# A hybrid decoder layer: one more projection unit in the fourth query blocks, and all gate chunks of a branch ahead of its products

## The chip, the cores and the metric

The kernel runs on one core of a Trainium2 chip. The metric is the device time of one execution in microseconds (us); before the change three runs gave a median of 1011.76 us, from 1009.65 to 1013.55. One more execution was profiled; its own time is given below.

## What is computed

One decoder layer of 512 tokens and width 1024, in float32, with a final RMSNorm. Cut to what matters here:

```
h = rms_norm(x)
fq, fk, fv, f_logit, dq, dk, dv, gate_a, gate_b = split(h @ w_in)
y_a = fox attention (8 heads of 64, causal, bias from the cumulative forget gate)
y_b = differential attention (4 heads: softmax(q1 k1) - lam * softmax(q2 k2), rotary q and k)
merged = sigmoid(gate_a) * (y_a @ w_branch_a) + sigmoid(gate_b) * (y_b @ w_branch_b)
x = x + merged @ w_out
x = x + cross_attention(rms_norm(x), rms_norm(mem))
x = x + mixture of 32 experts, 2 of 8 in one of 4 groups (SwiGLU, 512 wide)
out = rms_norm(x)
```

## The kernel before

The program is written in the order in which every engine carries it out: PE, DVE, ACT, POOL and the DMA queue of SP each take their instructions in the order of the text and wait only for semaphores. TensorE (PE) computes most products in three passes (high times high, high times low, low times high, lines 266 to 268), for which each weight is split in a high part (ACT, line 165) and a low part (POOL, or DVE for a few, line 166).

The first half is the mixer. All that is a projection of h is cut into *units*: one unit is 24 matmuls into one PSUM bank, with 128 columns of a weight chunk and all 512 tokens (`t_unit`, line 298), or 48 smaller ones (`nat_unit`, line 283). A unit returns its evacuation as a function, which is called later. The units stand in one list (lines 856 to 897), in the order: fox values, fox queries and keys of the second group (`fox_unit`), rotary queries and keys of the differential heads (`rope_unit`) with their values between, then for each branch its gate units (`gate_unit`, line 815) and its products (`branch_unit`, line 829: 12 matmuls with the attention's result). Before the change the order in a branch is two gate chunks (four units), four products, two gate chunks, four products; in branch B the memory's key/value units (`kv_unit`) stand ahead of the last four. The units of branch B also finish the merge: their evacuation takes L839 (gate times product) and L846 (sum of the two branches) on DVE, L849 on ACT and L850 on DVE.

The attention runs in 24 blocks (line 907): 16 of fox (four pairs of heads, four query blocks each; block 0 to 15) and 8 differential (two groups, four query blocks each; block 16 to 23). The query block b reads (b+1)*128 keys, so the fourth (b = 3, blocks 3, 7, 11, 15, 19, 23) is the longest. A block goes so (lines 918 to 963): scores on PE; softmax on DVE and ACT; whatever a rope unit left over (`late`: two matmuls with a swap matrix, L639 and L640, and its DVE and ACT steps); a unit; the product of the block before with its values; the combine step on DVE (L582 to L585, for differential L686 to L692), which scales the probabilities; the split of the next weight half (`W.more`); then the transposes of the probabilities on PE (L263) and their copies. In a differential block a second unit stands ahead of the transposes: the evacuation of the first is called there, then its rest, then the unit:

```
        if isinstance(it, Diff):
            ev()
            while late:
                late.pop(0)()
            ev = unit()
            W.more()
        it.trans()
```

PSUM banks come from three tags (line 74): units, rope rests and the transposes of the differential output (L738) share "a" with two banks; scores and transposes share "s" with four; "y" has two. SBUF is handed out in pages of 8 KB a partition, NPG = 18 of them (line 29): inputs, weights and results of the mixer, and later the experts' weights, which are fetched in a ring of 15 pages (`Experts`, line 1242) and two more tiles.

After the attention come the rest of the units (line 977), the output product (`out_unit`, line 999), the cross-attention, the router, and from about 520 us the loop over 16 pairs of experts (line 1553).

Of the kernel before, what the change touches and what calls it, by code (L numbers as in the profile page):

```python
# [21 lines left out]
NT = S // P  # L22
# [3 lines left out]
CAP = 64  # L26
QUAD = 4
NEG = -1.0e30
NPG = 18
NLD = 3  # L30
NPG2 = 4
RING = 15
# [6 lines left out]
def tile_hybrid_block(  # L39
# [7 lines left out]
    cp = ctx.enter_context(tc.tile_pool(name="cp", bufs=1))  # L47
    pgp = ctx.enter_context(tc.tile_pool(name="pgp", bufs=NPG))
    ps = ctx.enter_context(tc.tile_pool(name="ps", bufs=1, space=bass.MemoryType.PSUM))
# [6 lines left out]
    def page(shape, dt, name):  # L56
        return pgp.tile(list(shape), dt, name=name, tag="pg")
# [15 lines left out]
    def bank(name, tag):  # L73
        return ps.tile([P, 512], F32, name=name, tag=tag, bufs={"a": 2, "s": 4, "y": 2}[tag])
# [93 lines left out]
    W = Stream()  # L168

    def wcols(col):  # L170

        return W.add(w_inp[(col - 8 * (col > 1536)) // 256].rearrange("p (k n) -> p k n", k=KD), KD, 256)
# [97 lines left out]
    def gemm(o, nk, lh, ll, rh, rl):  # L270
        for k in range(nk):
            mm3(o, lh(k), ll(k), rh(k), rl(k), k == 0, k == nk - 1)
# [480 lines left out]
    def mem_load():  # L753
        M["x"] = page([P, 2, D], F32, "mt")
        nc.sync.dma_start(M["x"], mem[0].rearrange("(t p) d -> p t d", p=P))
        M["g"] = gvec(g_mem, "gb_mem")

    def mem_stat():
        ss = tiny([P, 2], "nm_ss")
        for t in range(2):  # L760
            junk = work([P, D], BF, f"nm{t}_j")
            A.activation(junk, M["x"][:, t], AF.Square, accum_out=ss[:, t:t + 1])
        M["r"] = rsqrt(ss, 2, 1.0 / D, 1e-6, "nm")

    def mem_norm(t):
        M["xn", t] = xn = big(f"nm{t}_n")
        V.scalar_tensor_tensor(xn, M["x"][:, t], M["r"][:, t:t + 1], M["g"], op0=OP.mult, op1=OP.mult)

    def mem_trans(t):
        if t == 0:  # L770
            M["h"] = page([P, KD, MEM], F32R, "mth")
            M["l"] = page([P, KD, MEM], F32R, "mtl")
        sl = slice(t * P, (t + 1) * P)
        for q in range(2):
            pt = bank(f"tm{t}{q}", "s")
            t4(pt, M["xn", t][:, q * 512:(q + 1) * 512])
            split(M["h"][:, 4 * q:4 * q + 4, sl], M["l"][:, 4 * q:4 * q + 4, sl],
                  pt.rearrange("p (a b) -> p a b", b=P))
        return None
# [3 lines left out]
    def kv_unit(i, j):  # L783
        if "k" not in M:
            M["k"] = page([P, 4, MEM], F32R, "kch")
            M["v"] = c2.tile([P, 2, MEM], F32, name="cv")
        wh, wl = W.use(c_kv[i], j)
        o = bank(f"kv{i}{j}", "a")[:, 0:256]
        sl = slice(j * P, (j + 1) * P)
        if i == 0:  # L790
            gemm(o, KD, lambda k: wh[:, k, sl], lambda k: wl[:, k, sl], lambda k: M["h"][:, k, :],
                 lambda k: M["l"][:, k, :])
        else:
            gemm(o, KD, lambda k: M["h"][:, k, sl], lambda k: M["l"][:, k, sl], lambda k: wh[:, k, :],
                 lambda k: wl[:, k, :])
        if i == 0:
            return lambda: split(M["k"][:, j], M["k"][:, 2 + j], o)
        return lambda: A.activation(M["v"][:, j], o, AF.Copy)

    wbr = [w[0].rearrange("(k p) n -> p k n", p=P) for w in (w_branch_a, w_branch_b)]  # L800
    c_ga, c_wa, c_gb, c_wb = [], [], [], []
    for c in range(4):
        c_ga.append(wcols(3080 + 256 * c))
        if c % 2 == 1:
            c_wa.append(W.add(wbr[0][:, :, 256 * (c - 1):256 * (c + 1)], 4, 512))
    for c in range(4):
        c_gb.append(wcols(4104 + 256 * c))
        if c == 3:
            for i in range(2):
                c_kv[i] = W.add(ckv[:, :, 256 * i:256 * i + 256], KD, 256)  # L810
        if c % 2 == 1:
            c_wb.append(W.add(wbr[1][:, :, 256 * (c - 1):256 * (c + 1)], 4, 512))
    GT = {}

    def gate_unit(br_, c, j):
        key = (br_, c // 2)
        if key not in GT:
            GT[key] = page([P, 4, S], F32, f"g{br_}{c // 2}")
        d = GT[key][:, 2 * (c % 2) + j]

        def evac(j, o):
            V.tensor_tensor(d, o, RT, op=OP.mult)
            A.activation(d, d, AF.Tanh, scale=0.5)

        return t_unit((c_ga, c_gb)[br_][c], j, evac, f"w{br_}{c}")
# [3 lines left out]
    def branch_unit(br_, c, j):  # L829

        wh, wl = W.use((c_wa, c_wb)[br_][c], j // 2)
        YH, YL = (YAH, YAL) if br_ == 0 else (YB["h"], YB["l"])
        o = bank(f"br{br_}{c}{j}", "a")
        sl = slice(j * P, (j + 1) * P)
        gemm(o, 4, lambda k: wh[:, k, sl], lambda k: wl[:, k, sl], lambda k: YH[:, k, :], lambda k: YL[:, k, :])

        def evac():
            ga = GT[br_, c][:, j]
            V.scalar_tensor_tensor(ga, ga, 1.0, o, op0=OP.add, op1=OP.mult)  # L839
            if br_ == 0:  # L840
                return
            if not MH:
                for i in range(2):
                    MH[i] = page([P, KD, S // 2], F32R, f"mh{i}")
                    ML[i] = page([P, KD, S // 2], F32R, f"ml{i}")
            V.tensor_tensor(ga, ga, GT[0, c][:, j], op=OP.add)  # L846
            for i in range(2):
                sl = slice(i * S // 2, (i + 1) * S // 2)
                A.activation(MH[i][:, 4 * c + j], ga[:, sl], AF.Copy, scale=0.5)  # L849
                V.scalar_tensor_tensor(ML[i][:, 4 * c + j], ga[:, sl], 0.5, MH[i][:, 4 * c + j].bitcast(F32),  # L850
                                       op0=OP.mult, op1=OP.subtract)

        return evac


    units = []
# [22 lines left out]
    for br_ in range(2):  # L879
        for c in range(4):  # L880
            for j in range(2):
                if (br_, c) == (1, 3):
                    units.append(lambda j=j: mem_trans(j))
                units.append(lambda br_=br_, c=c, j=j: gate_unit(br_, c, j))
            if (br_, c) == (0, 3):
                units.append(lambda: mem_load())
            if (br_, c) == (1, 0):
                units.append(lambda: mem_stat())
            if (br_, c) in ((1, 1), (1, 2)):
                units.append(lambda c=c: mem_norm(c - 1))  # L890
            if (br_, c) == (1, 3):
                for i in range(2):
                    for j in range(2):
                        units.append(lambda i=i, j=j: kv_unit(i, j))
            if c % 2 == 1:
                for j in range(4):
                    units.append(lambda br_=br_, c=c, j=j: branch_unit(br_, c // 2, j))
    wov = w_out[0].rearrange("(k p) n -> p k n", p=P)
    c_wo = [W.add(wov[:, :, 256 * c:256 * c + 256], KD, 256) for c in range(4)]
    c_cq = W.add(w_cq[0].rearrange("(k p) n -> p k n", p=P), KD, 256)  # L900
# [17 lines left out]
    for n, it in enumerate(its):  # L918
        it.scores()
        it.soft()  # L920
        while late:
            late.pop(0)()
        fe = rows() if rows is not None else None
        ev = unit()
        if fe is not None:
            fe()
        fin2 = prev.av() if prev is not None else None
        if n == 1:
            swap_matrix()
        if n == 2:  # L930
            rotary_angles()
        if n == 3:
            rotary_tables()
        if n == 4:
            lam_calc()
        if n == 5:
            rotary_spread()
        if n == 7:
            dv = page([P, NT, 512], F32, "dv")
        it.combine()  # L940
        if fin is not None and isinstance(done, Diff):
            done.scale()
        W.more()
        if isinstance(it, Diff):
            ev()
            while late:
                late.pop(0)()
# [4 lines that stand above are left out]
            it.copy()  # L952
            ev()
        else:
            ev()
            it.copy()
        rows = fin
        if isinstance(it, Fox) and it.b == NT - 1 and it.pr < 3:
            Fox(it.pr + 1, 0).prep()
        if n == 15:  # L960
            YB["h"] = page([P, 4, S], F32R, "ybh")
            YB["l"] = page([P, 4, S], F32R, "ybl")
        done, prev, fin = prev, it, fin2
# [807 lines left out]
```

## Time and profile before

| | us |
|---|---|
| median of three runs | 1011.76 |
| lowest, highest | 1009.65, 1013.55 |
| the profiled execution | 1016.84 |
| its span (first to last instruction) | 1015.1 |

In the profile PE is TensorE's matmuls, PEld its weight loads, DVE is VectorE, ACT ScalarE, POOL GpSimd and SP the engine whose queue issues the DMAs. "L692" is line 692 of the kernel. An idle mark at the end of a row, such as `[1.01 <-DVE T L692]`, tells how long the engine stood idle ahead of this instruction and what ended that. PEclk is the granted share of TensorE's full clock of 2.4 GHz.

### The profile page before, as it was taken

The page shows a single profiled execution, that of the slowest core. Times are in us where ns is not written, and L with a number is a line of the kernel's source. Part 1 is how long each engine was busy: PE and PEld are TensorE (multiplying, and loading weights), DVE is VectorE, ACT ScalarE, POOL GpSimd, SP SyncE. Part 2 cuts the span into 40 slices and gives each one's busy share as a digit, 9 for nine tenths or more (in the row PEclk, how much of TensorE's full clock was granted, in tenths as well). Part 3 has the DMA queues.
Part 4 walks back from the last instruction along what each step waited for, and adds up shares of the span by engine and source line. Part 5 has one row for each costly group of instructions (what it writes and reads, how often), then busy time and mean ns, then how long its engine had stood idle before and what let it go on. Part 6 is the DMA issues. An engine that isn't in the chain of part 4 may idle for free. (4 is left out here: it accounts for less than half of the span.)

```text
span 1015.1 us, 13870 instructions
## 1 busy us (share of the span) xinstructions
PE 968.5 (95%) x5494; PEld 643.9 (63%) x5495; DVE 453.9 (45%) x966; ACT 307.7 (30%) x670; POOL 195.9 (19%) x244
## 2 busy tenths in 40 slices
PE   7999899999999999999899999999999999999985
PEld 6687677787877888898656536354363635436332
DVE  5455685846563535445632333322333332233334
ACT  5334344434352344345421202121021212112104
POOL 3840222233343455610100000000000000000003
PEclk9999999999899999999999999999999999999998
DMA  8121121112132228336479899999999999999902
GB/s 305 63 84 63 42 62 64 63 63 81 45 115 86 90 85 270 122 126 274 183 279 419 314 423 421 421 421 418 421 422 421 422 420 421 420 421 420 409 18 83
DMA packets 47575, 246.19 MB, mean 243 GB/s; under 512 B 4625, under 2 KB 12049, under 8 KB 23441
## 3 DMA queue, kind: packets, MB, share of 16 engines
q1 hardware_dynamic: 47360, 245.03, 61.0%
q8 instruction: 45, 0.74, 0.3%
q14 instruction: 26, 0.20, 0.1%
q10 hardware_dynamic: 144, 0.21, 0.1%
HBM read 243.13 MB, written 2.10 MB: 242 GB/s over the span
## 5 line engine op out<-in xcount | busy, mean ns | idle before, releaser
L1403 PE MATMUL gu<-gu,xg 128*64 128x512 f32 x960 | 210.5, 593 | 1.7 <-PEq L1472 1.6
L166 POOL TENSOR_TENSOR wl<-wr,wh 128x1024 fp32r<-128x1024 f32 x50 | 120.4, 2414 | 194.2 <-ACT wh L165 187.0
L1403 PEld LDWEIGHTS gu<-gu,xg 128*64 128x64 f32 x960 | 72.8, 137 | 133.3 <-issue 118.6
L1425 PE MATMUL yd<-dn,A 128*64 128x512 f32 x472 | 110.4, 596 | 0.0
L1447 DVE TENSOR_TENSOR xr<-cb,xr 128x512 f32<-128x512 f32 x120 | 75.7, 685 | 50.7 <-PE cb L1443 50.5
L1408 DVE SCALAR_TENSOR_TENSOR A<-A,gu 128x256 f32<-128x256 f32 x32 | 13.5, 421 | 176.1 <-ACT A L1407 176.1
L1543 POOL MEMSET A<- 128x128 f32 x1 | 0.2, 205 | 438.2 <-PE pth L263 438.2
L1425 PEld LDWEIGHTS yd<-dn,A 128*64 128x64 f32 x472 | 34.9, 137 | 64.4 <-issue 63.4
L1407 ACT ACTIVATE A<-gu 128x256 f32<-128x256 f32 x32 | 12.3, 383 | 200.7 <-PE gu L1403 200.7
L165 ACT ACTIVATE wh<-wr 128x1024 fp32r<-128x1024 f32 x64 | 66.8, 1050 | 7.7 <-POOL wr L135 6.8
L1443 PE MATMUL cb<-Y,ohT 128*128 128x512 f32 x240 | 66.7, 408 | 0.9
L1433 DVE SCALAR_TENSOR_TENSOR Y<-yd,ws,Y 128x512 fp32r<-128x512 f32 x32 | 23.9, 751 | 91.8 <-ACT Y L1432 89.9
L1231 PE MATMUL ga<-G,hnh 128*128 128x256 f32 x256 | 64.6, 290 | 0.2 <-DVE ge L1351 0.2
L1231 PE MATMUL ga<-G,hnl 128*128 128x256 f32 x256 | 62.8, 283 | 0.0
L1432 ACT ACTIVATE Y<-yd,ws 128x512 fp32r<-128x512 f32 x32 | 21.9, 687 | 126.9 <-PE yd L1425 126.9
L1231 PEld LDWEIGHTS ga<-G,hnh 128*128 128x128 f32 x256 | 48.6, 190 | 3.1 <-issue 2.4
L1443 PEld LDWEIGHTS cb<-Y,ohT 128*128 128x128 f32 x240 | 42.1, 189 | 12.3 <-DVE xr L1447 3.4
L1231 PEld LDWEIGHTS ga<-G,hnl 128*128 128x128 f32 x256 | 48.6, 190 | 0.6
L1377 ACT ACTIVATE xg<-ga,smc 128x256 f32<-128x256 f32 x64 | 29.8, 474 | 52.3 <-PE ga L1231 52.3
L266 PE MATMUL wop<-wh,mh 128*128 128x256 f32 x128 | 36.9, 288 | 3.0 <-DVE xr L1011 1.8
L267 PE MATMUL wop<-wl,mh 128*128 128x256 f32 x128 | 36.4, 284 | 0.5 <-POOL wl L166 0.5
L268 PE MATMUL wop<-wh,ml 128*128 128x256 f32 x128 | 36.4, 284 | 0.0
(611 smaller groups left out, 1958.8 us busy)
## 6 DMA issues: line engine op xcount, KB each, us to landing
gu<-in_w_gu_dram SPq DMA_DIRECT2D x120, 1024.0 KB, 12.1
dn<-in_w_dn_dram SPq DMA_DIRECT2D x55, 1024.0 KB, 17.2
wr<-in_w_inp_dram SPq DMA_DIRECT2D x40, 512.0 KB, 3.7
Z<-in_w_gu_dram SPq DMA_DIRECT2D x8, 1024.0 KB, 14.6
wr<-in_w_out_dram SPq DMA_DIRECT2D x8, 512.0 KB, 5.6
Z<-in_w_dn_dram SPq DMA_DIRECT2D x4, 1024.0 KB, 19.8
dn<-in_w_dn_dram SPq DMA_DIRECT2D x6, 512.0 KB, 13.9
xT<-in_x_t_dram SPq DMA_DIRECT2D x4, 512.0 KB, 6.8
```

What stands on the lines that cost most here:

```text
L165: A.activation(hi, src, AF.Copy)
L166: E.tensor_tensor(lo, src, hi.bitcast(F32), op=OP.subtract)
L266: PE.matmul(o, lh, rh, start=first, stop=False)
L267: PE.matmul(o, lh, rl, start=False, stop=False)
L268: PE.matmul(o, ll, rh, start=False, stop=last)
L1231: PE.matmul(o, CX[u, t // 2][:, t % 2, kb * P:(kb + 1) * P], GQ[q][:, t].rearrange("p e s -> p (e s)"), start=(first and u == "h"), stop=( ...
L1377: A.activation(XG[q][:, kb], o, AF.Copy, scale=gfc[:, kb:kb + 1])
L1403: PE.matmul(gu[64 * f:64 * f + 64, :], xg(2 * i + j), w[:, :, j, 256 * f:256 * f + 256], start=(i + j == 0), stop=(i + j == 4))
L1425: PE.matmul(y[j][64 * a:64 * a + 64, :], hT[a][:, f % 2, f // 2], w(a, f)[:, j, f % 2], start=(f == 0), stop=(f == 3))
L1433: V.scalar_tensor_tensor(yl[rows, j], y[j][rows], ws, yh[rows, j].bitcast(F32), op0=OP.mult, op1=OP.subtract)
L1443: PE.matmul(banks[j], oh[:, t * P:(t + 1) * P], y[u][:, j], start=(u == 0), stop=(u == 1))
L1447: V.tensor_tensor(xs, banks[j], xs, op=OP.add)
```

## The change

Three things. A fourth query block of either kind goes once more through the step that stood in differential blocks alone: evacuation, rest, unit, split. So fourth fox blocks have two units between scores and transposes and fourth differential blocks three. The list of units (and of weight chunks, which must agree) has all four gate chunks of a branch ahead of its eight products. And there is one page more, since more gate results are alive at once.

```diff
-NPG = 18
+NPG = 19
...
     for c in range(4):
         c_ga.append(wcols(3080 + 256 * c))
-        if c % 2 == 1:
-            c_wa.append(W.add(wbr[0][:, :, 256 * (c - 1):256 * (c + 1)], 4, 512))
+    for c in range(2):
+        c_wa.append(W.add(wbr[0][:, :, 512 * c:512 * c + 512], 4, 512))
     for c in range(4):
         c_gb.append(wcols(4104 + 256 * c))
         if c == 3:
             for i in range(2):
                 c_kv[i] = W.add(ckv[:, :, 256 * i:256 * i + 256], KD, 256)
-        if c % 2 == 1:
-            c_wb.append(W.add(wbr[1][:, :, 256 * (c - 1):256 * (c + 1)], 4, 512))
+    for c in range(2):
+        c_wb.append(W.add(wbr[1][:, :, 512 * c:512 * c + 512], 4, 512))
...
-            if c % 2 == 1:
+            for c2_ in ((), (0, 1))[c == 3]:
                 for j in range(4):
-                    units.append(lambda br_=br_, c=c, j=j: branch_unit(br_, c // 2, j))
+                    units.append(lambda br_=br_, c=c2_, j=j: branch_unit(br_, c, j))
...
-        if isinstance(it, Diff):
+
+        for _ in range(isinstance(it, Diff) + (it.b == NT - 1)):
             ev()
             while late:
                 late.pop(0)()
```

## Rows read from the trace of the kernel before

**Rows 1.** The page: busy us, share of span, instructions; PE's slices in tenths.
```profile
PE 968.5 (95%) x5494; PEld 643.9 (63%) x5495; DVE 453.9 (45%) x966; ACT 307.7 (30%) x670; POOL 195.9 (19%) x244
...
PE   7999899999999999999899999999999999999985
```
**Rows 2.** Stretches: us, busy of PE PEld DVE ACT POOL, clock, DMA share, GB/s.
```profile
600.00:650.00 50.00, 50.00 (x269) 24.20 (x266) 13.00 (x25) 8.64 (x18) 0.00 (x0) 1.00 1.01 421
```
**Rows 3.** Order of time, PE, block 19: start us, us, engine, line, op, [idle before].
```profile
243.26 0.40 PE L666 MATMUL sd<-maskb,identb 128*128 128x128 bf16 x4
...
247.72 0.47 PE L266 MATMUL br<-yah,wh 128*128 128x512 f32 x1
...
250.34 0.39 PE L268 MATMUL br<-yah,wl 128*128 128x512 f32 x1
251.74 0.63 PE L263 MATMUL td<-identf,T 128*128 128x128 f32 x4 [1.01 <-DVE T L692]
252.93 0.63 PE L263 MATMUL td<-identf,T 128*128 128x128 f32 x4 [0.56 <-DVE T L692]
```
**Rows 4.** Order of time, PE, end of block 23 and behind it.
```profile
304.20 0.63 PE L263 MATMUL td<-identf,T 128*128 128x128 f32 x4 [1.04 <-DVE T L692]
...
306.48 0.66 PE L738 MATMUL tz<-identf,zn 128*128 128x128 f32 x4 [0.48 <-DVE g L839]
307.68 0.50 PE L266 MATMUL br<-yah,wh 128*128 128x512 f32 x1 [0.54 <-DVE g L839]
```
**Rows 5.** Order of time, PE: block 7 (three rows), blocks 11 and 15.
```profile
118.87 0.39 PE L266 MATMUL dq0p<-hh,wh 128*128 128x512 f32 x1
...
124.40 0.88 PE L607 MATMUL yo<-pf,fv 128*64 128x128 f32 x12
...
126.23 0.66 PE L263 MATMUL tf<-identf,S 128*128 128x128 f32 x4 [0.36 <-DVE S L585]
...
161.17 1.09 PE L263 MATMUL tf<-identf,S 128*128 128x128 f32 x8
...
196.74 0.66 PE L263 MATMUL tf<-identf,S 128*128 128x128 f32 x4 [0.31 <-DVE S L585]
```
**Rows 6.** Stretches behind blocks 15, 19 and 23; the clock is third from the end.
```profile
199.10:202.50 3.40, 3.40 (x17) 3.21 (x18) 2.79 (x10) 1.77 (x9) 0.00 (x0) 0.50 0.05 18
...
253.70:260.50 6.80, 6.80 (x29) 5.60 (x28) 4.83 (x17) 2.67 (x10) 0.00 (x0) 0.50 0.05 18
...
308.30:311.70 3.40, 3.40 (x10) 2.63 (x9) 0.65 (x1) 0.00 (x0) 1.74 (x1) 0.50 0.11 19
```
**Rows 7.** Order of time, DVE, combine of block 19 and the next evacuation.
```profile
248.67 2.92 DVE L692 SCALAR_TENSOR_TENSOR T<-T,dr,T 128x512 f32<-128x512 f32 x1
...
252.03 0.75 DVE L692 SCALAR_TENSOR_TENSOR T<-T,dr,T 128x512 f32<-128x512 f32 x1
...
253.30 0.68 DVE L839 SCALAR_TENSOR_TENSOR g<-g,br 128x512 f32<-128x512 f32 x1
```
**Rows 8.** Order of time, POOL, block 19.
```profile
248.67 2.38 POOL L166 TENSOR_TENSOR wl<-wr,wh 128x1024 fp32r<-128x1024 f32 x1 [3.28 <-DVE T L691]
```
**Rows 9.** Order of time, DVE, evacuation of block 7's rope unit.
```profile
126.09 0.68 DVE L166 TENSOR_TENSOR dqk0l<-dq0p,dqk0h 128x512 fp32r<-128x512 f32 x1
126.69 0.68 DVE L635 TENSOR_TENSOR r001a<-dq0p,rot 128x512 f32<-128x512 f32 x1
```
**Rows 10.** Order of time, PE, transposes of the third blocks 6 and 14.
```profile
116.85 0.55 PE L263 MATMUL tf<-identf,S 128*128 128x128 f32 x3 [1.13 <-DVE S L585]
...
187.43 0.55 PE L263 MATMUL tf<-identf,S 128*128 128x128 f32 x3 [0.79 <-DVE S L585]
```
**Rows 11.** Branch B's evacuation: a group (busy us, mean ns, idle), an instruction in time.
```profile
L846 DVE TENSOR_TENSOR g<-g,g 128x512 f32<-128x512 f32 x8 | 13.9, 1732 | 0.3
...
398.46 0.76 DVE L850 SCALAR_TENSOR_TENSOR ml<-g,mh 128x256 fp32r<-128x256 f32 x2 [0.48 <-ACT mh L849]
```
**Rows 12.** Order of time, PE, the output product behind branch B.
```profile
399.87 0.39 PE L266 MATMUL wop<-wh,mh 128*128 128x256 f32 x1 [0.55 <-DVE g L839]
```

## The prediction

> **What bounds the kernel now.** I read the page first. TensorE (PE) is busy 95% of the span, and its row of slices is at nine tenths nearly everywhere [rows 1]. So a change pays only where it takes away PE idle time or slow PE clock. Then I looked at the second half by stretches: in 600 to 650 us, which stands for all of 525 to 950, PE is busy 50.00 of 50 us while the DMA engines are also full (1.01, 421 GB/s) [rows 2]. There the weights stream just fast enough, and PE never stops. The change touches nothing that PE does there, so whatever the attention part wins or loses moves the end by the same amount.
>
> Then I went through PE's own order of time in the attention part (58 to 316 us) and wrote down each idle mark and what ended it. Blocks are numbered 0 to 23 in the order of the loop; 3, 7, 11 and 15 are the fourth query blocks of fox, 19 and 23 those of the differential heads. In block 19 the scores end at 243.66, two branch products of 3.0 us each run (247.72 to 250.73 is the second), and then PE waits 1.01 us for the first transposes and 0.56 us for the second [rows 3]. Both waits end with DVE at L692. Block 23 repeats this (1.04, and again 0.56), and loses 0.48 and 0.54 us more just behind it, waiting for L839 on DVE [rows 4]. In fox, block 7 waits 0.36 and block 15 0.31 us, block 11 nothing [rows 5]. The stretches give the other loss: after blocks 15, 19 and 23 the granted clock is 0.5, which is 1.2 instead of 2.4 GHz, for 3.4, 6.8 and 3.4 us, with PE busy all the time [rows 6]. Half of that is lost: 1.7 + 3.4 + 1.7 = 6.8 us. So what the change aims at is 1.6 + 2.6 + 0.7 us of waiting and up to 6.8 us of slow clock, 11.7 us, of which it has to pay its own costs.
>
> **Why DVE is late there.** The combine step's L692 took 2.92 us in block 19; the same instruction on the other half took 0.75 [rows 7]. Next to it POOL ran the weight split of the next unit, from 248.67 to 251.05 [rows 8]. The long one ended half a microsecond behind the split's end. The Trainium skill, SBUF — State Buffer, "Who interferes with whom", has a rule for this: DVE's second port is GpSimd's, it is an exclusive lock, and the loser stands until the other's instruction is over. The trace agrees (2.92 against 0.75 us). By that rule the extra unit speaks against itself in part, because each new weight half brings another such split.
>
> **The change part by part.**
>
> *Block 23 and what is behind it.* Now three units stand between scores and transposes, and by the new order they are three gate units; a unit of 24 matmuls takes 5.5 us (118.87 to 124.40) [rows 5]. The last combine ends 9.1 us behind the scores (243.66 to 252.78 in block 19 [rows 3, 7]), and the first two gate units alone take 11. So all four waits go, 1.04 + 0.56 + 0.48 + 0.54 = 2.62 us. I leave 0.2 for the wait of the next unit on the third one's evacuation: **-2.4**.
>
> *Block 19.* Here the three units are products of branch A, 3.0 us each, and the third is not free to start. Projections share two PSUM banks (tag "a"), so the third needs the bank of the first. The first is emptied by L839, and DVE works in order: in the code that step stands behind combine. In the trace it ran from 253.30 to 253.98, behind L692 and the scaling [rows 7]. PE is through with the second unit at 250.73 [rows 3]. So PE waits 3.3 us ahead of the third unit, where it waited 1.57 ahead of the transposes: **+1.7**. Queued behind that wait on PE are the transposes, the next block's scores and all that follows. If DVE had that bank free earlier it would be -1.6; that is the lower end.
>
> *Blocks 7 and 11.* Their extra unit comes behind another rope unit (unit order: by then one and two units have been taken early, so block 7 holds both of group 0's last key units, block 11 a query and a key unit of group 1). The new pass empties the first, and runs its rest, which is two matmuls with the swap matrix, before the second unit. These read what ACT and DVE have just split. In block 7 DVE did that split at 126.09 to 126.77 and freed the bank with L635 at 127.37 [rows 9], while PE is free from 125.28 (124.40 + 0.88) [rows 5]. The first swap matmul (0.4 us) goes at once, the second waits for 126.77, the unit for 127.37: about 1.3 us idle in place of 0.36 in block 7 and of none in block 11. **+0.9 and +1.3.** Lower end 0 each, if the split comes early; upper end 2 each.
>
> *Blocks 3 and 15.* Block 3 has a fox unit and then a fox unit, and no wait now: nothing. Block 15 gets two gate units, and its 0.31 us goes: **-0.3**.
>
> *The shift of units.* From block 4 on each block has a later unit than now. In the third blocks of fox, a rope unit alone went with a wait of 1.13 us and a rope unit behind another with 0.79 [rows 10]; these change places among blocks 6, 10 and 14. I count **0**, from -1 to +1. The moved memory load (two DMAs on SP's queue, now in block 19 instead of 23) lies well ahead of its use and behind short weight loads: 0. The memory statistics move into block 23; their ACT and POOL work hides under gate units.
>
> *Branch B's eight products in one row.* Before, four products stood between gate units and four behind the key/value units. Now all eight stand together behind those. On PE one takes 3.0 us [rows 3]. On DVE one takes L839 0.68 [rows 7], L846 1.73 in the mean of eight [rows 11], 0.48 us of waiting for ACT and L850 0.76 for the pair [rows 11]: 3.65 us, less some tenths of overlap, 3.4. The mean of L846 holds free and blocked ones: it adds two tiles that both lie in SBUF, as L692 does, and stands still beside a split. Over four products DVE falls behind by some 2 us and PE feels it only in the output product, where it waits 0.55 for L839 [rows 12] and about as long once more. Over eight, DVE enters the last four already late by this much and two banks are all that PE has in hand. Working through the queue (products 1 to 8, split on 1, 3, 5, 7, 8), the last one's evacuation ends about 3.5 us later than now against PE's work, and the output product needs it: **+3.5**. From 1 (if DVE catches up in the first four) to 5.5 (a sixth blocked addition).
>
> *The clock.* With block 15's and 23's waits gone I expect their slow stretches to go: **-1.7 and -1.7**. Behind block 19 the wait doubles, so some slow clock stays; it had 6.8 us, in part because transposes and short scores followed, and a full unit will follow now. Between 0 and -1.7: I take **-0.9**. New ones could come at blocks 7 and 11 and among the eight products; waits of 1.1 us there now (116.85) [rows 10] had none behind them, so 0, up to +1.7 each.
>
> *The 19th page.* It holds the fourth gate tile. If it also lets the expert ring run one page ahead, a page is 1 MB at 421 GB/s, 2.5 us earlier on a stream that PE does not wait for [rows 2]: **0**.
>
> Sum: -2.4 + 1.7 + 0.9 + 1.3 - 0.3 + 0 + 3.5 - 1.7 - 1.7 - 0.9 = **+0.4 us**. The profiled execution took 1016.84 us, of which the span is 1015.1; the median of the runs shown is 1011.76, 5.1 us less. I carry the difference over to the median: **1012.2**.
>
> **The rivals.**
>
> *It does what it says.* If the third unit in block 19 is not held by the bank, nor blocks 7 and 11 by the rope rest, then all waits go (1.6 + 2.4 + 0.7) and all the slow clock (6.8), and only branch B is paid: -11.5 + 3.5 = -8, **1004**. For it: the waits are there and have that size. Against: two banks and DVE's order are plain in the rows [rows 7, 9].
>
> *The clock does not come back and falls in new places: slower.* Place: the joints of blocks 7, 11, 15, 19, 23. It decides once a new wait of over a microsecond lies against transposes and short scores, as in blocks 19 and 23 now [rows 3, 4]. The forecast's 4.3 us of clock are then not won, and two stretches of 3.4 us come behind blocks 7 and 11, 1.7 us each: 1012.2 + 4.3 + 3.4 = **1020**. For it: block 15 lost its clock with a wait of only 0.31 us. Against: block 7 with 0.36 did not [rows 5].
>
> *The 19th page helps the stream.* The ring ahead by one page gives up to 2.5 us, **1009.7**; against it stands PE's full row [rows 2].
>
> **How the numbers follow.** Forecast (waits traded for waits, clock partly won) 0.6; does what it says 0.12; clock lost 0.23; page 0.05. A measurement of this kernel tells about 0.5%, 5 us, from no change. Faster by more: the second case, 0.12, and nothing of the forecast's own lower end (1012.2 - 2.5 for branch B - 2 for the rope blocks - 0.8 for clock = 1007). Slower by more: the clock case and a little of the forecast's upper end, 0.23. Else the same, 0.65. The forecast's own range is 1007 to 1016; out to the others, so that two in ten stay out, 1006.5 to 1018.5.
>
> **What would show it.** In PE's order of time: no idle mark ahead of the transposes of blocks 15, 19 and 23; in block 19 an idle of about 3 us ahead of the third branch product, ended by L839; in blocks 7 and 11 about 1 us ahead of the second swap matmul (L640), ended by DVE L166; among branch B's products waits for L839, and the output product later. In the clock: no 0.5 behind blocks 15 and 23. Wrong would be an idle-free block 19, eight products without a wait on DVE, or another pace in the expert loop.

## The result and the profile after

The changed kernel takes **1028.95 us** (median of five runs, 1028.79 to 1031.0), against 1011.76 before (five runs, 1009.65 to 1013.55): a ratio of 1.017, 95% interval 1.0151 to 1.0189. It is slower by 17 us. The forecast was 1012.2, and its range ended at 1018.5.

The profiled execution after took 1028.95 us with a span of 1027.2. That is 12.1 us more than the profiled execution before, though the medians differ by 17.2; the missing 5.1 us come up again below. The first view is the page: PE's busy time, and its slices in tenths, to be held against [rows 1].

```profile
PE 969.4 (94%) x5494; PEld 644.9 (63%) x5495; DVE 465.1 (45%) x966; ACT 307.3 (30%) x670; POOL 198.8 (19%) x244
...
PE   7999999999799998799889999999999999999985
```

PE is busy for as long as before (969.4 against 968.5 us). The 12 us are new idle time, and the slices show where: the 11th (257 to 283 us) and the 16th and 17th (385 to 437 us) have fallen below nine tenths. (The router shows in the 20th and 21st; before it showed in the 20th alone.) The next two rows are the stretches after. The first runs from the attention's first matmul to the transposes of the ranks (L1466) at the head of the expert loop, the second from there to the end (columns: us, busy time of PE PEld DVE ACT POOL, clock, DMA share, GB/s).

```profile
57.15:531.06 473.91, 441.19 (x2823) 369.79 (x2822) 272.60 (x597) 194.97 (x437) 151.90 (x160) 0.98 0.31 107
531.06:1027.20 496.14, 478.70 (x2415) 233.69 (x2412) 162.36 (x312) 87.56 (x187) 8.79 (x19) 0.99 0.91 374
```

The same two stretches before:

```profile
58.56:519.23 460.67, 440.62 (x2822) 370.03 (x2822) 262.05 (x597) 195.38 (x437) 149.89 (x160) 0.98 0.31 109
519.23:1015.10 495.87, 478.60 (x2415) 233.76 (x2412) 162.31 (x312) 87.58 (x187) 8.80 (x19) 0.99 0.91 375
```

So the second half took 495.87 and then 496.14 us: the experts go on at their pace, as forecast. The first stretch is 13.2 us longer, of which 12.7 are idle time of PE (473.91 - 441.19 = 32.7, against 20.05). The attention began 1.4 us earlier; I don't count that to the change, as in three profiles whose code is the same up to there (before, again, before59) it began between 57.1 and 60.0 us. The two largest marks are in block 19 and in the output product.

**Block 19** (scores end at 266.3; compare [rows 3, 7, 8]). PE, then DVE, then POOL, in order of time:

```profile
272.94 0.39 PE L268 MATMUL br<-yah,wl 128*128 128x512 f32 x1
278.74 0.80 PE L266 MATMUL br<-yah,wh 128*128 128x512 f32 x1 [5.41 <-DVE g L839]
```

```profile
270.76 0.49 DVE L691 TENSOR_SCALAR T<-T,dm 128x512 f32<-128x512 f32 x1
271.28 2.94 DVE L692 SCALAR_TENSOR_TENSOR T<-T,dr,T 128x512 f32<-128x512 f32 x1
274.15 2.56 DVE L691 TENSOR_SCALAR T<-T,dm 128x512 f32<-128x512 f32 x1
276.74 0.75 DVE L692 SCALAR_TENSOR_TENSOR T<-T,dr,T 128x512 f32<-128x512 f32 x1
277.41 0.68 DVE L729 TENSOR_TENSOR zn<-zo,rq_z 128x512 f32<-128x512 f32 x1
278.01 1.28 DVE L839 SCALAR_TENSOR_TENSOR g<-g,br 128x512 f32<-128x512 f32 x2
```

```profile
271.27 2.40 POOL L166 TENSOR_TENSOR wl<-wr,wh 128x1024 fp32r<-128x1024 f32 x1 [3.29 <-ACT wh L165]
...
273.62 2.81 POOL L166 TENSOR_TENSOR wl<-wr,wh 128x1024 fp32r<-128x1024 f32 x1
```

The third product waits for L839 on DVE, as forecast, but 5.41 us and not 3.3. POOL makes two splits in a row here, where it made one before. So not only is L692 long (2.94 us), the L691 behind it is too: 2.56 us against 0.49 for the same instruction just ahead. Each of the two long ones ends some tenths behind the end of a split: L692 at 274.22 and the first split at 273.67, L691 at 276.71 and the second split at 276.43. No idle mark stands ahead of them, so this is no wait for a semaphore: the time is within the instruction.

**The output product** (from 412 us before, from 416 now). DVE, POOL and PE after:

```profile
415.91 11.45 DVE L166 TENSOR_TENSOR wl<-wr,wh 128x1024 fp32r<-128x1024 f32 x1
427.28 0.74 DVE L1012 TENSOR_TENSOR xr<-wop,xr 128x256 f32<-128x256 f32 x2
```

```profile
413.21 4.75 POOL L166 TENSOR_TENSOR wl<-wr,wh 128x1024 fp32r<-128x1024 f32 x2
417.93 3.74 POOL L135 TENSOR_TENSOR wr<-wr,sma 128x1024 f32<-128x1024 f32 x2
421.64 4.63 POOL L166 TENSOR_TENSOR wl<-wr,wh 128x1024 fp32r<-128x1024 f32 x2
```

```profile
427.84 0.55 PE L266 MATMUL wop<-wh,mh 128*128 128x256 f32 x1 [6.28 <-DVE xr L1012]
```

And the kernel before in the same place: DVE, then POOL, then what POOL's queue itself waited for (columns of the last row: line, queue, instruction, count, shortest/median/longest ns, first and last start).

```profile
411.75 6.81 DVE L166 TENSOR_TENSOR wl<-wr,wh 128x1024 fp32r<-128x1024 f32 x1
418.48 0.74 DVE L1011 TENSOR_TENSOR xr<-wop,xr 128x256 f32<-128x256 f32 x2
```

```profile
413.74 3.74 POOL L135 TENSOR_TENSOR wr<-wr,sma 128x1024 f32<-128x1024 f32 x2
418.70 4.75 POOL L166 TENSOR_TENSOR wl<-wr,wh 128x1024 fp32r<-128x1024 f32 x2 [1.22 <-ACT wh L165]
```

```profile
L166 POOLq EVENT_SEMAPHORE  x1: 7825/7825/7825, 410.8 to 410.8; - x1
```

One weight split (the second half of chunk `c_wo[3]`, number 59 in the stream) is given to DVE by line 113. It lies between two additions (L1012) that free the banks of the output product. Before, it took 6.81 us, and PE waited 1.68 us for it. Now it takes 11.45, and PE waits 6.28. In both kernels POOL works beside it: two splits, two scalings of `c_cq` (L135), two splits. After the change they follow one another without a pause; before, POOL stood still for 1.22 us at 417.5. The label there names ACT, but the queue's own wait began at 410.8 and lasted 7.825 us, to 418.6: that is where DVE's split ends (411.75 + 6.81 = 418.56). POOL waited for DVE's split, and in that pause DVE got it done. No row of the profile names the page, but in the code the only thing that POOL's next split needs from DVE's is a page of SBUF that DVE has still to read; the runs with 18 and 19 pages below decide it. After the change POOL's queue has no such wait there, and DVE's split ends 1.1 us behind POOL's last one (421.64 + 4.63 = 426.27; 415.91 + 11.45 = 427.36).

**The joints behind the fourth fox blocks** (where one block ends and the next one's scores begin), PE and then DVE behind block 3, then PE behind block 7 (block 11 has the same 0.74):

```profile
94.86 0.32 PE L536 MATMUL sf<-fqk0h 64*128 64x128 f32 x1 [0.39 <-ACT pf L596]
95.71 0.32 PE L536 MATMUL sf<-fqk0h 64*128 64x128 f32 x1 [0.53 <-DVE pf L596]
...
92.97 0.69 DVE L379 TENSOR_TENSOR fn<-fk1p,RT 128x512 f32<-128x512 f32 x1 [4.41 <-PE fk1p L268]
94.36 0.69 DVE L381 SCALAR_TENSOR_TENSOR fqk1l<-fn,fqk1h 128x512 fp32r<-128x512 f32 x1 [0.70 <-ACT fqk1h L380]
94.97 0.68 DVE L596 COPY pf<-tf 128x512 f32<-128x512 f32 x1
...
140.92 0.32 PE L536 MATMUL sf<-fqk1h 64*128 64x128 f32 x1 [0.74 <-DVE pf L596]
```

The last unit now ends just ahead of the transposes, and in fox blocks its evacuation (L379 and L381 here) is called ahead of the copies of the transposes (L596). So the copy that frees a bank for the next block's scores starts late, and PE waits. The forecast had nothing here.

The other marks, from the same order of time (block numbers as in the forecast; PE's idle time in us):

| place | before | after | forecast | measured |
|---|---|---|---|---|
| joint behind block 3 | 0 | 0.39 + 0.53 | 0 | +0.9 |
| block 7 (L640) and its joint | 0.36 + 0.14 | 1.02 + 0.10 + 0.74 | +0.9 | +1.4 |
| block 11 (L640) and its joint | 0 | 1.07 + 0.10 + 0.74 | +1.3 | +1.9 |
| third fox blocks 6, 10, 14 | 1.13 + 0.51 + 0.79 | 0.75 + 0.49 + 0.23 | 0 | -1.0 |
| block 15 and its joint | 0.31 + 0.19 + 0.14 | 0.22 | -0.3 | -0.4 |
| block 19 | 1.01 + 0.56 | 5.41 | +1.7 | +3.8 |
| block 21 and the scores and the gate unit behind it | 0 | 0.90 + 0.31 + 0.66 | 0 | +1.9 |
| block 23 and behind it | 2.62 + 0.35 | 0.60 | -2.4 | -2.4 |
| branch B's products | 0.55 + 0.56 + 0.17 + 0.54 | 1.57 + 0.36 + 0.55 + 0.56 + 0.22 + 0.49 | +3.5 | +1.9 |
| output product, additions | 1.68 | 6.28 | 0 | +4.6 |

The measured column sums to 12.6 of the 12.7 us; marks that are the same in both kernels and single ones of up to 0.14 us in other places are not in the table. The slow clock is not gone. Two of its three stretches after:

```profile
276.10:282.90 6.80, 4.16 (x10) 3.29 (x11) 3.15 (x5) 0.00 (x0) 0.32 (x1) 0.50 0.31 97
426.20:433.00 6.80, 5.16 (x24) 5.19 (x25) 1.82 (x3) 0.00 (x0) 0.07 (x1) 0.50 0.46 154
```

They lie at the two long waits. Block 19 had one of this length before too; the one in the output product is new. A third, at 508.2 in the router, has 4.94 us of busy time at half clock. Together (4.16 + 5.16 + 4.94) / 2 = 7.1 us are lost, against 8.5 before (17.0 us of busy time at half clock behind blocks 15, 19 and 23 and in the router at 499.4).

### The profile page after: what moved, and what is told of

Read it like the earlier page. It is cut to its first block, busy times and chain, and to the rows that moved or that the text cites. A ratio compares the mean times of both kernels' runs of the same rounds, so it can differ in the third digit from the quotient of the medians.

```text
span 1027.2 us, 13862 instructions
## 1 busy us (share of the span) xinstructions
PE 969.4 (94%) x5494; PEld 644.9 (63%) x5495; DVE 465.1 (45%) x966; ACT 307.3 (30%) x670; POOL 198.8 (19%) x244
## 5 line engine op out<-in xcount | busy, mean ns | idle before, releaser
L166 POOL TENSOR_TENSOR wl<-wr,wh 128x1024 fp32r<-128x1024 f32 x50 | 121.5, 2437 | 203.3 <-ACT wh L165 203.3
## 6 DMA issues: line engine op xcount, KB each, us to landing
gu<-in_w_gu_dram SPq DMA_DIRECT2D x120, 1024.0 KB, 12.6
dn<-in_w_dn_dram SPq DMA_DIRECT2D x55, 1024.0 KB, 17.2
```

The costliest lines, as they stand in the source:

```text
L166: E.tensor_tensor(lo, src, hi.bitcast(F32), op=OP.subtract)
```

## The experiments

Two theories stood first. **The page:** the 19th page takes away POOL's pause, and the output product pays. **The order:** eight products in a row bring DVE late to its split, and the page has no part in it. All ratios are to the kernel before, with a 95% interval. It was measured anew beside each group of runs (the first four below; late_split, ev_first, copy_first and best_a; again, before59 and b_order; mended), with medians of 1012.16, 1013.07, 1011.72 and 1012.2 us. So a difference between runs of different groups is known to 1 or 2 us only, and that goes for every difference from the changed kernel too, which was not measured again.

### The page alone

The kernel before with one line changed:

```diff
-NPG = 18
+NPG = 19
```

> The kernel before with NPG = 19 and nothing else. Theory P (the page): with 18 pages POOL's first split of c_cq has to wait for a page that DVE's split of c_wo[3] was the last to read; that pause of 1.2 us on POOL is when DVE gets its split done. With a 19th page POOL goes on, DVE's split takes about 11.4 us instead of 6.8, PE waits about 6.3 us instead of 1.7 in the output product and may lose 3.4 us more of clock behind it: 1016 to 1020 us. Rival Q (the order: eight products in a row bring DVE late to its split): the page alone changes nothing, 1012 +- 1.5 us, PE's wait there 1.7 us.

Measured: 1018.54 us, ratio 1.0068 (1.0047 to 1.0089). DVE, POOL and PE in the output product:

```profile
407.42 11.41 DVE L166 TENSOR_TENSOR wl<-wr,wh 128x1024 fp32r<-128x1024 f32 x1
...
409.40 3.73 POOL L135 TENSOR_TENSOR wr<-wr,sma 128x1024 f32<-128x1024 f32 x2
413.11 4.63 POOL L166 TENSOR_TENSOR wl<-wr,wh 128x1024 fp32r<-128x1024 f32 x2
...
419.31 0.55 PE L266 MATMUL wop<-wh,mh 128*128 128x256 f32 x1 [6.28 <-DVE xr L1011]
```

No pause on POOL, 11.41 us for the split, and the same wait of 6.28 us, with the old order of units. The page alone costs 6.4 us: the wait is 4.6 us longer, and from 415.7 us PE ran at half clock for 6.8 us, of which it was busy for 3.19. The order theory fell.

### The changed kernel with 18 pages

```diff
-NPG = 19
+NPG = 18
```

> The changed kernel with NPG = 18 again: order of units and extra passes as changed, the page taken back. Theory P: POOL's wait for the page is back, DVE's split takes about 7 us, PE waits about 1.7 us in the output product, no slow clock behind it: 1029 - 4.6 - 3.4 = 1021 us, or 1024 if the clock falls all the same. Rival Q: 1029 us, and PE's wait of 6.3 us stays. A page fewer may also hold up loads elsewhere; then new waits of PE for weight halves show.

Measured: 1023.69 us, 1.0122 (1.0101 to 1.0144), 5.3 less than the changed kernel. POOL and DVE:

```profile
418.49 3.74 POOL L135 TENSOR_TENSOR wr<-wr,sma 128x1024 f32<-128x1024 f32 x2
423.45 2.39 POOL L166 TENSOR_TENSOR wl<-wr,wh 128x1024 fp32r<-128x1024 f32 x1 [1.22 <-ACT wh L165]
...
416.46 6.85 DVE L166 TENSOR_TENSOR wl<-wr,wh 128x1024 fp32r<-128x1024 f32 x1
423.24 0.74 DVE L1012 TENSOR_TENSOR xr<-wop,xr 128x256 f32<-128x256 f32 x2
```

The pause of 1.22 us is back and the split is at 6.85 us again; PE waits 1.68. No new wait for a weight came with the page fewer. The change's units did not need that page.

### The split on POOL

```diff
-            self.pool = set(range(12, 64)) - {57, 59}
+            self.pool = set(range(12, 64)) - {57}
```

> The changed kernel, with the low part of c_wo[3]'s second half made by POOL instead of DVE (set of halves for POOL without the exception of 59). If DVE's 11.45 us split is what PE waits for in the output product, DVE has its additions free, the wait of 6.28 us goes and the slow clock behind it too: 1029 - 6.3 - 3.4 = 1019 us. Rival: PE then waits for POOL's split itself (POOL does three in a row, the third out some 7 us after the first starts): a wait of 1 to 3 us stays, 1021 to 1024 us.

Measured: 1020.37 us, 1.0086 (1.0066 to 1.0106): 8.6 us less than the changed kernel, with its 19 pages. PE has no wait in that place at all, and no slow clock. DVE's addition now waits for PE:

```profile
419.32 0.42 DVE L1012 TENSOR_TENSOR xr<-wop,xr 128x256 f32<-128x256 f32 x1 [2.73 <-PE wop L268]
```

### The order without the extra pass

```diff
-        for _ in range(isinstance(it, Diff) + (it.b == NT - 1)):
+        for _ in range(isinstance(it, Diff)):
```

> The changed kernel without the extra passes: the new order of gate units and products and the 19th page alone, one pass in differential blocks, none in fox blocks. Theory P: the output product loses 4.6 us to the page and 3.4 to clock, branch B's eight products 2 us, blocks 19 and 23 are as before: 1012 + 10 = 1022 us. If instead the passes themselves (block 19's wait of 5.4 us, the joints behind fox fourth blocks) carry most of the loss: 1014 us or less.

Measured: 1019.94 us, 1.0084 (1.0063 to 1.0104), neither of the two figures by itself. With the page alone at 1018.54, the order of units adds 1.4 us, which lies within the spread of the runs of either, and the extra passes (1028.95 - 1019.94) **9.0**. So page 6.4, order 1.4, passes 9.0, put in one after the other. The next runs are about the passes. In this run block 19 holds two gate units, and PE stands nowhere in it: the order by itself does what the pass was to do there.

### Block 19: one split instead of two

In the changed kernel:

```diff
-        for _ in range(isinstance(it, Diff) + (it.b == NT - 1)):
+        for k_ in range(isinstance(it, Diff) + (it.b == NT - 1)):
...
             ev = unit()
-            W.more()
+            if (n, k_) != (19, 1):
+                W.more()
```

> The changed kernel, with the last weight split of block 19 (the one that the extra pass queues) left to block 20. Theory: POOL then makes one split beside block 19's combine instead of two in a row, so only L692 is long (2.9 us) and L691 behind it takes 0.5 instead of 2.56; PE's wait ahead of the third product is 3.3 us, the figure forecast, instead of 5.4: 1029 - 2.1 = 1027 us, and 1023.5 if the slow clock behind it goes too. Rival: the wait is not DVE's queue behind POOL but something else of the third product; then it stays at 5.4 us.

Measured: 1035.18 us, 1.021 (1.0187 to 1.0232), 6.2 slower than the changed kernel. The wait did what was expected of it; DVE, then PE, then POOL:

```profile
274.30 2.93 DVE L692 SCALAR_TENSOR_TENSOR T<-T,dr,T 128x512 f32<-128x512 f32 x1
277.15 0.47 DVE L691 TENSOR_SCALAR T<-T,dm 128x512 f32<-128x512 f32 x1
...
279.66 0.80 PE L266 MATMUL br<-yah,wh 128*128 128x512 f32 x1 [3.29 <-DVE g L839]
...
300.40 0.79 PE L268 MATMUL br<-yah,wl 128*128 128x512 f32 x1 [4.52 <-POOL wl L166]
...
294.23 0.19 POOL L218 TENSOR_SCALAR rq_v<-s 128x4 f32<-128x4 f32 x1 [17.55 <-ACT sj L722]
...
298.01 4.66 POOL L166 TENSOR_TENSOR wl<-wr,wh 128x1024 fp32r<-128x1024 f32 x2
```

L691 takes 0.47 us and the wait is 3.29: the forecast's 3.3. The second split is the other 2.1 us. But the split moved behind the small operations of the output norm on POOL, which wait 17.55 us for ACT, and came out at 300.3. PE waited 0.78 and 4.52 us for that weight, with a slow stretch of 6.8 us from 299.5. (The profile is of the slowest of the six runs, 1039.13 us.) POOL's early start was no luxury.

### Block 19: the bank freed ahead of the combine step

In the changed kernel:

```diff
+        if n == 19:
+            ev()
+            ev = lambda: None
         it.combine()
```

> The changed kernel, with the evacuation of block 19's first product put ahead of the combine step on DVE. Theory: the third product waits for that bank alone, so it now starts straight behind the second; the transposes behind it wait for L692 as before the change, some 2 us. 5.4 us become 2, and the slow clock behind is shorter by up to 3.4 us of half speed: 1029 - 3.4 - (0 to 1.7) = 1024 to 1025.6 us. Rival: the bank is not what holds the product: wait and time stay, 1029 us.

Measured: 1023.87 us, 1.0103 (1.0081 to 1.0124), 5.1 less. DVE's evacuation and what PE still waits for:

```profile
270.87 0.69 DVE L839 SCALAR_TENSOR_TENSOR g<-g,br 128x512 f32<-128x512 f32 x1
...
279.26 0.63 PE L263 MATMUL td<-identf,T 128*128 128x128 f32 x4 [1.17 <-DVE T L692]
280.96 0.33 PE L536 MATMUL sd<-dqk1h 64*128 64x128 f32 x2 [0.60 <-DVE pd L704]
```

The third product starts at once; 1.17 + 0.60 are left of 5.41. The slow stretch is 3.4 us instead of 6.8. So the bank was what held the third product.

### The copies first in fourth fox blocks

In the changed kernel:

```diff
-        if isinstance(it, Diff):
+        if isinstance(it, Diff) or it.b == NT - 1:
             it.copy()
             ev()
```

> The changed kernel, with the copies of the transposes ahead of the last unit's evacuation in fourth fox blocks too (as in differential blocks). Theory: the waits of PE in the scores behind blocks 3, 7 and 11 (0.39 + 0.53, 0.74, 0.74 us) come from copies that queue behind the evacuation of a unit that ended just ahead of the transposes; they go: 1029 - 2.4 = 1026.6 us. Rival: the evacuation is then late for the bank of the next unit and the wait only moves: 1029 us.

Measured: 1024.82 us, 1.0123 (1.0099 to 1.0148), 4.1 less. The waits behind blocks 3, 7 and 11 are gone; in their place came 0.17 us (ended by DVE's L166) and 0.09 us behind blocks 7 and 11 each. That explains some 2 of the 4.1; its profile has no slow stretch at 508, but whether that belongs to this edit no run tells.

### All three repairs

The changed kernel with 18 pages, the split on POOL, the early evacuation of block 19 and the copies first: the four edits above in one. What is left of the change is the extra pass and the order.

> The changed kernel with all three repairs: 18 pages and c_wo[3]'s second half split by POOL, copies ahead of the evacuation in fourth fox blocks, the first product's evacuation ahead of the combine step in block 19. What is left is the extra pass itself; the comparison is the run b_order (1012.0 us), which has the same order and the same split but no extra pass. By the idle marks: 26.3 us of PE idle time from 58 us to the router in the changed kernel, less 6.28, less 2.4, less 3.6, is 14.0, against 13.8 in b_order: 1012 us, so the extra pass gives nothing even when it is mended. If the extra pass is worth what it removes (the waits of blocks 15 and 23, 3 us), 1009 us. If the three repairs don't add up, 1016 us or more.

Measured: 1012.73 us, 0.9996 (0.998 to 1.0012). The three repairs take away 16.2 us together, where alone they took 8.6, 5.1 and 4.1, and the kernel stands where the same order without a pass stands (1012.02, next run). PE waits 1.18 and 0.60 us in block 19, with no slow clock behind. So the extra pass, even if it is made as it should be, gives nothing that these runs can tell from none; a difference under some 2 us they don't show.

### The order of branch B

A version with 18 pages, the split on POOL, no extra pass and the new order in both branches. It differs from the version below (best_a) in branch B's order alone (and in the order of its weight chunks, which must agree and isn't shown).

```diff
-            for c2_ in ((), (c // 2,))[c % 2] if br_ else ((), (0, 1))[c == 3]:
+            for c2_ in ((), (0, 1))[c == 3]:
```

> The version of the run best_a (1008.7 us), with branch B's gates ahead of its products as in the change. The price of eight products in a row by itself: the forecast had 3.5 us, from 1 to 5.5; the idle marks of the changed kernel say 1.9. 1010.6 us by the marks, 1012.2 by the forecast, and up to 1.7 us more with a slow stretch of clock.

Measured: 1012.02 us, 0.9999 (0.9985 to 1.0014). Against 1008.72 that is 3.3 us for eight products in a row, where the forecast had 3.5. The two runs are of different groups: by their ratios to the kernel before (0.9999 and 0.995) it is 5.0 us. The marks alone, 1.9, fall short of either.

### The version that beats both

18 pages, no extra pass, the split on POOL, and the new order for branch A only. Two places of it, against the kernel before:

```diff
-            self.pool = set(range(12, 64)) - {57, 59}
+            self.pool = set(range(12, 64)) - {57}
...
-            if c % 2 == 1:
+            for c2_ in ((), (c // 2,))[c % 2] if br_ else ((), (0, 1))[c == 3]:
```

> A version to beat both: 18 pages, no extra pass, the new order of gates and products for branch A alone, branch B as before the change, and the second half of c_wo[3] split by POOL. Against the kernel before: the output product's 1.68 us and block 19's 1.57 us of waiting go, and with them 0 to 3.4 us of slow clock; two waits of 0.67 us come with branch A's products (as they stand in the run with the order alone). 1012.2 - 1.9 - (0 to 3.4) = 1007 to 1010 us. Rival: the moved products lose as much in other places: 1012 us.

Measured: 1008.72 us, 0.995 (0.9929 to 0.9972): faster than the kernel before by 0.5%, in the range expected. The median of the kernel before was the highest of the four groups here, 1013.07; against the lowest, 1011.72, the gain is 3.0 us.

### The split alone

The kernel before with the same line 113 as above, and nothing else.

> The kernel before, with the second half of c_wo[3] split by POOL instead of DVE, and nothing else. DVE's split of 6.8 us goes and with it PE's 1.68 us in the output product; POOL's wait for the page goes with it, as POOL then reads that page itself: 1012.2 - 1.7 = 1010.5 us. Rival: POOL is late with it by then and PE waits for POOL: 1012 us or more.

Measured: 1010.48 us, 0.999 (0.9971 to 1.0009). PE's wait of 1.68 us is gone from its profile, but the time can't be told from no change.

### The kernel before once more

Nothing changed.

> The kernel before once more, for a second profile. The first one took 1016.84 us, 5.1 above the median of the runs. Theory: it had slow clock behind blocks 15 and 19 (1.7 + 3.4 us lost) that a usual execution of the same code does not have; this profile then shows no half clock at about 199 and 254 us, with the same waits of PE there, and a time of 1011 to 1013 us. The forecast's gain of 4.3 us of clock was then for the most part never to be had against the median. Rival: the slow stretches belong to the waits and come again; then the 5.1 us lie somewhere else, ahead of the attention for instance.

Measured: 1018.17 us for this one profiled execution. The theory fell: both slow stretches are there again. The rows of this second profile, and then of the run before59, which is the same program up to 400 us:

```profile
200.70:204.10 3.40, 3.40 (x17) 3.21 (x15) 2.79 (x10) 1.92 (x9) 0.00 (x0) 0.50 0.04 16
255.30:262.10 6.80, 6.70 (x28) 5.41 (x27) 4.80 (x18) 2.56 (x10) 0.00 (x0) 0.50 0.04 13
```

```profile
195.50:202.30 6.80, 6.46 (x55) 5.86 (x55) 5.05 (x15) 3.62 (x11) 0.00 (x0) 1.00 0.27 77
250.20:257.00 6.80, 6.53 (x49) 5.50 (x48) 5.24 (x18) 2.79 (x10) 0.00 (x0) 1.00 0.13 47
```

The same blocks, with the same waits of 0.3 and 1.55 to 1.58 us, ran at half clock in two profiles and at full clock in before59 and in the run with the page alone. So these stretches are no fixed part of the program. Nor is the one behind block 23: this second profile has none there, with the four waits of 2.6 us in place. A profile of the kernel before without them, at its median, there is not. But every run has its mean granted clock on record, and over the 65 runs of the kernel before the time goes with it: a median of 1016.4 us in the 7 runs at 0.983 and less, 1013.6 in the 14 at 0.985 and 0.986, 1012.2 in the 31 at 0.987 and 0.988, 1010.2 in the 13 above. Both profiled executions stand at 0.983. So the 5.1 us by which the first lies above the median go with its clock; that they are just the stretches behind 15 and 19 is likely by their size (1.7 + 3.4) and not shown.

## Why the prediction was wrong, step by step

**"The 19th page: 0."** This step failed most dearly: +6.4 us. I asked what a page more would let start earlier, found the stream of weights full, and stopped. I did not ask which waits the missing page had made. One of them was of use: POOL waiting for DVE is DVE getting its turn. The forecast had the mechanism in hand (L692 and POOL's split [rows 7, 8]) and even wrote that each new split speaks against the change, but it did not look for DVE's own split at L166, whose 6.81 us before the change stood in the trace.

**"Block 19: +1.7."** Place, waiting instruction and cause were right: the third product waits for its bank, the bank for L839, and L839 stands behind the combine step (the run ev_first). The term was mis-sized, +3.8: it held one POOL split beside the combine step, and there are two. With one, the run late_split showed 3.29 us. The pass that adds a unit also adds the split of the next weight half, and POOL makes it as soon as ACT has the high part, long ahead of its place on PE. It must be counted beside DVE's work at that time.

**"Blocks 7 and 11: +0.9 and +1.3."** The waits ahead of the second swap matmul came as written, 1.02 and 1.07 us, ended by DVE's L166. What I left out were the joints: the unit's evacuation stands ahead of the copies in fox blocks, 2.4 us with block 3, for which I had "nothing". I followed PE up to the transposes and not on to who needs their banks.

**"The shift of units: 0."** The third blocks gave 1.0 back, which was the end of that range. But four products of branch A moved from block 23 and behind it to blocks 19, 21 and 22, where two of 3.0 us (block 21) cover less than two gate units of 5.5: in block 21 and behind it PE waits 1.9 us. That undoes most of what block 23 gains. **Block 23** itself went as forecast: its four waits are gone.

**"Branch B: +3.5."** Measured 3.3 to 5.0 by itself. The mechanism is in the trace too: L846 takes 2.8 to 2.9 us for four of the eight additions and 0.69 to 0.88 for the others, and PE waits 1.57 us for L839 among the products. Two of the additions:

```profile
396.69 0.69 DVE L846 TENSOR_TENSOR g<-g,g 128x512 f32<-128x512 f32 x1
399.25 2.86 DVE L846 TENSOR_TENSOR g<-g,g 128x512 f32<-128x512 f32 x1
```

**"The clock: -4.3."** No stretch stands behind 15 and 23, as forecast, but that may be luck: behind 15 in the runs page19 and before59, and behind 23 in the run again, the clock stayed full with the waits in place. Block 19's share, -0.9, was not won: its stretch is 6.8 us as before, with the third product behind the wait in place of the transposes. That short work had made it long, as the forecast said, no run shows. And a new stretch came in the output product; 1.4 us of 8.5 were won in the profile. Worse was the sum: I carried the 5.1 us between profile and median over to the forecast, and took 4.3 us for clock that the median may not have lost. The same microseconds can't be won twice. The profile after lies at its median, so the real difference of medians, 17.2, is 12.1 of the profiles and these 5.1. The granted clock says the same: 0.982 to 0.983 in the five runs of the changed kernel, 0.987 to 0.988 at the median of the kernel before, 0.983 in its profile.

**The rivals.** The slower one (1020) had the right sign and less than half of the size. That 4.3 us of clock would not be won came true in the medians; its two stretches behind blocks 7 and 11 did not come, and it had nothing of the 12.7 us of new idle time. The forecast's chance of 0.23 for slower was too low because each part was priced against the work that stands beside it before the change.

## What to carry to other kernels

A wait that a resource causes may be doing work: before adding a buffer, look in the queue's own waits for who gets a turn while it lasts, above all with two engines that block each other. When a unit is added to a place, count everything it issues on other engines, and there in the order in which those engines reach it (here a second split on POOL beside the combine step), and follow the freed banks one step further than the instruction you want to move. Where a profiled execution lies outside the runs, don't win back losses that only it shows.

## What the runs showed of the hardware that I had not expected

A DVE instruction that met POOL's splits did not always wait for one of them only. In the output product it stood through a row of splits and scalings without getting in between them: 11.45 us after and 11.41 with the page alone, where the other half that DVE splits (411.95 to 413.18 after) took 1.23 us, and it ended 1.1 us behind POOL's last. With a pause of 1.22 us on POOL it needed 6.81 and 6.85. The Trainium skill, SBUF — State Buffer, "Who interferes with whom", says that the loser blocks for the whole instruction of the other; the traces agree. In the output product they add that POOL's next instruction, which followed at once, went ahead of the DVE instruction that was already standing there, four times in a row. It is not always so: in block 19 DVE's L692 ended 0.55 us behind the first split, and the second split, already begun by the profile, took 2.81 us in place of 2.40 (in ev_first 2.83). There DVE got its turn in between. What decides which of the two happens no run shows.

The granted clock was 0.5, 1.2 instead of 2.4 GHz, at each of the ten waits of PE of 5.4 and 6.28 us: in block 19 in the changed kernel and in after18, pool59 and copy_first, and in the output product in all six profiles that have the wait there. Behind block 19's waits of 1.6 to 1.8 us in sum it came in some profiles (before, again, ev_first) and not in others (page19, before59, mended).
